# Three-product gate and query tiles, with their lower halves made by transfers or by GpSimd

## The chip, the cores and the metric

The kernel runs on one core of a Trainium2 chip. A core has five engines with queues of their own: TensorE (matrix products, PE in the profile, with PEld for its weight loads), VectorE (DVE), ScalarE (ACT), GpSimd (POOL) and SyncE (SP), whose queue issues transfers. The metric is the device time of one execution in microseconds (us); the time before is the median of three runs.

## The reference, cut to what matters

Two layers, each a mixer block and an expert block, over 16 meta tokens and 256 tokens of width 1024 in float32.

```
def _mixer_block(x, ...):
    h = _rmsnorm(x, mix_g)
    z = h @ w_in                      # conv input, query, kv, rope, gate logits
    u = conv_in[..., :D_CONV] * sigmoid(conv_in[..., D_CONV:])
    u = _causal_depthwise_conv(u, conv_w, conv_b)          # 31 taps, 512 channels
    u = silu(_layernorm(u, conv_ln_g, conv_ln_b))
    y_conv = u @ w_conv_out
    ...                               # multi-head latent attention -> o
    y_mla = o @ w_mla_out
    gates = sigmoid(gate_logits)      # 2 x 1024 columns of z
    merged = gates[..., :D_MODEL] * y_conv + gates[..., D_MODEL:] * y_mla
    return x + merged @ w_out

def _peer(h, wq, keys, u_table, v_table):
    q = (hf @ wq).reshape(T, 8 heads, 2, 128)
    s = einsum('thpd,hpnd->thpn', q, keys)                 # 128 keys each
    sv, si = top_k(s, 16);  top_s, top_pos = top_k(sums of pairs, 16)
    gw = softmax(top_s)
    a = einsum('ted,td->te', u_table[experts], xb)
    return einsum('te,ted->td', gelu(a) * gw, v_table[experts])
```

There are 16,384 experts of width 1024 in each of the tables u and v.

## The kernel before, in words

The program holds the whole model in one run, layer after layer. Layer 0 works on all 272 columns (tokens), layer 1 on the 256 of the output from the mixer's gates on. TensorE takes weights as 128 x 1024 tiles: eight blocks of 128 x 128, one for each 128 rows of the input, against 272 or 256 columns.

**Weights.** They stream in as 1 MB loads of two tiles each, in a list (`srcs`, `raws`), through a ring of buffers `wraw`. `next_w` (L104) hands out the next tile and, at every second one, has SP issue the loads further on in the ring (`dma_to`, L82). `peek_w(n)` (L99) gives a tile that lies n places ahead. In the query stage some loads of the expert table u are taken out of the ring and issued early, at tiles named in `EPLACE` (L35); four of them go into buffers borrowed from mixer tiles (`kh`, `sq`, `g0`, `g1`).

**The two forms of a product.** `ztile` (L298) multiplies a tile in f32: eight matmuls, each of which shows as two in the trace, 16 in all. `three` (L721) has the weight as a sum of two f32r numbers, hi and lo, and the input as xh + xl, and adds the three products hi·xh, lo·xh and hi·xl: 24 matmuls of one pass each. The halves of a weight are made ahead by `high` (L688) and `low` (L713). `high` has ScalarE copy the tile to the type f32r (L709). `low` makes w - hi in one of three ways: by VectorE or GpSimd as a subtraction (L719), or by a transfer, where ScalarE first writes -w rounded the same way (L711) and GpSimd's queue then issues a transfer from w that adds to it (L717). `kinds` (L685) names the buffers of each split tile; they are mixer buffers that are free at that time.

**Order in the mixer.** All engines follow one program text. After the first four tiles come four pairs of conv-input tiles (loop over c, L817), where at c = 2 the normalised input is split into xh (`uk`, L839) and xl, then 16 gate tiles (L859; `TPG`, L29, lists those in three products: 10 to 15), four tiles for y_mla, four for y_conv, and eight of w_out. Attention (`att`) and the convolution are generators, and the text advances them by a fixed number of steps behind each tile: `taps(n, m)` does n conv taps on VectorE (`conv`, L649) and m steps of `conv2` (L665). The 31 taps of a channel block are a multiplication and 30 multiply-adds on VectorE (L661). Of channel block 0 the first KD = 21 taps go another way: ScalarE writes scaled copies, three at a time, accumulating transfers on GpSimd's queue add them up in `part`, and three VectorE additions put them into `acc`. They run as soon as VectorE has begun block 0. `TAPS` (L27) sets the taps of each gate tile. When all taps are done, `layernorm` (L744) starts: sums on VectorE (L747), a product with ones on TensorE, and so on; its steps are placed in the later gate tiles.

**Order in the query stage.** 16 query tiles (L1156) in two-half form from 0 to 11 (tile 16 + i in `parts`; 12 to 15 are f32). Behind the product of a tile the text makes the halves of tiles 3 or 4 ahead (the dictionary at L1163), issues an early load if `EPLACE` has the place, evacuates z to `qr` by ScalarE (L1172), computes the scores of the tile before on TensorE, and picks the best 16 of each by `top16` on VectorE (L1003). From tile 12 on ScalarE copies the scores out (L1029), so TensorE doesn't wait for VectorE's picks. At i = 4 to 11 GpSimd also makes xh, the input of the expert stage (L1205). The steps of `heads(0, 0)` (candidates, exponentials, indices) run in i = 8 to 14 on VectorE; then `numbers` (L1145) computes the expert numbers, and SP moves them to `iww` by `spread` (L1150).

**The expert stage.** 128 tiles of u (product A, L1483) and then 128 of v (product po). Alongside, GpSimd gathers single rows of u by the expert numbers and VectorE reduces them (L1440, L1425); routes come from them through VectorE (L1308) and TensorE transposes (L1319).

Of the kernel before, what the change touches and what calls it, by code (L numbers as in the profile page):

```python
# [7 lines left out]
F32 = mybir.dt.float32  # L8
# [5 lines left out]
OP = mybir.AluOpType  # L14
# [8 lines left out]
KW = 31  # L23
# [3 lines left out]
TAPS = [6, 6, 7, 8] + [9] * 12  # L27
KD = 21
TPG = (10, 11, 12, 13, 14, 15)  # L29
SCALE = 96 ** -0.5  # L30
# [6 lines left out]
MIXQ = {"xg", "uk", "qr", "rq_w", "rq_x", "rq_ym", "tkw0", "tkw1", "tkw2", "tkm", "sk", "scs", "qm",  # L37
        "wq0", "wq1", "seln", "upad", "acc", "sqa", "g0", "g1"}
# [15 lines left out]
def trunk_kernel(ctx: ExitStack, tc: tile.TileContext, a: dict, out: bass.AP, dbg=None, stop=None):  # L54
    nc = tc.nc
# [156 lines left out]
    for l in range(NL):  # L212
# [16 lines left out]
        mixs = ExitStack()  # L229
        mixb = ExitStack()  # L230
        mpa = mixs.enter_context(tc.tile_pool(name=f"mixq{l}", bufs=1))
        mpb = mixb.enter_context(tc.tile_pool(name=f"mix{l}", bufs=1))

        class mp:

            @staticmethod
            def tile(shape, dt, name, **kw):
                return (tw if name in ("sq", "kh", "g0", "g1") else mpa if name in MIXQ else mpb).tile(shape, dt, name=name, **kw)
        zs = ExitStack()
# [425 lines left out]
        def conv2():  # L665

            for k in range(0, KD, 3):
                u_ = mp.tile([128, 3, T], F32, name="cp", bufs=2) if k else part
                for x in range(3):
                    S.activation(u_[:, x, t0:], upad[:, 0, k + x + t0:k + x + T], AF.Copy, scale=weight(0, k + x))  # L670
                    yield
                if k:
                    G.dma_start(part[:, :, t0:], u_[:, :, t0:], accum_op=OP.add)
            for _ in range(2):
                yield
            while ck[0] == KD:
# [3 lines left out]
            yield  # L680

        parts = {}

        xhs_ = []
        kinds = {"g10": 0, "g11": 1, "g12": "k", "g13": 0, "g14": 1, "g15": "s", 0: "k", 1: 0, 2: 1, 3: "s", 4: "k",  # L685
                 19: "k", 20: "a", 21: "q", 22: "w", 23: "s", 24: "q", 25: "a", 26: "s", 27: "w"}

        def high(i, n):  # L688

            w_ = peek_w(n)  # L690
            x = kinds[i] if i in kinds else "aws"[(i - 5) % 3]
            if x == "w":
                hi, lo = [mp.tile([128, 1024], F32, name=f"wq{y}") for y in range(2)]
# [15 lines left out]
            S.activation(parts[i][0], w_, AF.Copy)  # L709
            if i in (21, 23, 25, 27):  # L710
                S.activation(parts[i][1], w_, AF.Copy, scale=-1.0)  # L711

        def low(i):  # L713

            hi, lo, w_ = parts[i]
            if i in (21, 23, 25, 27):
                G.dma_start(lo, w_, accum_op=OP.add)  # L717
            else:
                (G if i in (20, 22, 24, 26) else V).tensor_tensor(lo, w_, hi.bitcast(F32), op=OP.subtract)  # L719

        def three(i, p, xs, wc, cs, first, end, mid=None):  # L721

            hi, lo, _ = parts[i]
            for c in cs:
# [92 lines left out]
        for c in range(4):  # L817
# [17 lines left out]
            if c == 2:  # L835
                xnh = big("uk", [8, T], F32R)
                xnl = mp.tile([128, 8, T], F32, name="un").bitcast(F32R)
                for k in range(8):
                    S.activation(xnh[:, k, t0:], xg[:, k, t0:], AF.Copy)  # L839
# [19 lines left out]
        for i in range(16):  # L859
# [4 lines left out]
            else:  # L864
                z = ztile(t0)
            new = [f"g{i + 2}"] if i + 2 in TPG else []
            ns = [1] if new else []
# [7 lines left out]
            if not ex:  # L875
                todo.append(i)
            if i >= 14:
                high(i - 12, 3)
# [102 lines left out]
        normal(7)  # L981
        mixb.close()
        if stop == f"mix{l}":
            dump(stop, hT)
# [171 lines left out]
        for i in range(16):  # L1156
# [4 lines left out]
            else:  # L1161
                z = ztile(t0)
            for k in {0: (2, 3), 1: (5,), 2: (4,), 3: (7,), 4: (6,), 5: (9,), 6: (8,), 7: (11,), 8: (10,)}.get(i, ()):  # L1163
                high(16 + k, k - i - 1)
                low(16 + k)
            if i in EPLACE:
                k, n = early_[l][EPLACE[i][0]], EPLACE[i][1]
                raws[k] = (two(n).rearrange("p (a b) -> p a b", a=2) if n else
                           ep.tile([128, 2, 1024], F32, name=f"we{i}"))
                nc.sync.dma_start(raws[k], srcs[k])  # L1170
            qT_ = mp.tile([128, T], F32, name="qr", bufs=2)
# [578 lines left out]
```

## Time and profile before

| | us |
|---|---|
| median of three runs (lowest, highest) | 1659.36 (1658.32, 1661.72) |
| the profiled execution | 1659.62 |
| its span | 1657.8 |
| TensorE busy | 1642.4 |
| VectorE busy | 1261.6 |
| ScalarE busy | 693.3 |
| GpSimd busy | 333.0 |

The profiled execution is one run recorded by the hardware. A row of a timeline reads: start and duration in us, engine, line of the program, operation, the written and the read tile, the form; in square brackets how long the engine stood before it and what ended that. A row of the chain of waits has start, duration, engine, tile and line, and the number of instructions. In the windows each engine's busy us stand with its count of instructions, then the granted TensorE clock, the busy share of the 16 transfer engines and the GB/s that they moved. Matmul ends are modelled, and transfers are listed with the median time from issue to landing.

### The profile page before, as it was taken

Reading aid. Unit: us, or ns where it says so; the run is one execution under the profiler, and the core shown is the slowest. Engines: PE = TensorE matmul, PEld = TensorE weight load, DVE = VectorE, ACT = ScalarE, POOL = GpSimd, SP = SyncE. Lnnn points to the kernel's source line nnn. Section 1 sums busy time; section 2 is a strip of 40 time slices with the busy share of each in tenths; the row PEclk is TensorE's granted clock in tenths of the full one; section 3 lists DMA queues with packets and bytes.
Section 4 is the critical chain, followed back from the end, with each engine's and each line's share of the span. In section 5 each row is a group of like instructions: output and inputs, shape, how many; then the busy total and the mean of one; then the engine's idle time right before and its main releaser. Section 6 shows DMA issues by size and latency. Waiting matters only on the chain.

```text
span 1657.8 us, 30712 instructions
## 1 busy us (share of the span) xinstructions
PE 1642.4 (99%) x11827; PEld 1468.5 (89%) x11827; DVE 1261.6 (76%) x3082; ACT 693.3 (42%) x1803; POOL 333.0 (20%) x347
## 2 busy tenths in 40 slices
PE   9999999999999999999999999999999999999999
PEld 7679999999999999999986899999999997566655
DVE  5799899897898544444447998897877886788885
ACT  3565733435554111000024576433445443455554
POOL 0000033221222222222200100432211222233330
PEclk9999999999999999999999999999999999999999
DMA  6444697999999999999962746989999999999994
GB/s 249 113 128 177 242 345 298 424 383 424 416 423 418 424 424 423 424 424 424 417 259 85 176 153 242 340 348 396 362 425 409 409 391 411 420 425 425 424 425 191
DMA packets 86099, 568.52 MB, mean 343 GB/s; under 512 B 10328, under 2 KB 15384, under 8 KB 18744
## 3 DMA queue, kind: packets, MB, share of 16 engines
q1 hardware_dynamic: 50608, 338.51, 50.7%
q0 software_dynamic: 34560, 227.31, 35.0%
q8 instruction: 93, 1.52, 0.4%
q10 hardware_dynamic: 784, 0.74, 0.1%
q14 instruction: 54, 0.44, 0.1%
HBM read 556.18 MB, written 1.05 MB: 336 GB/s over the span
## 4 chain that ended last, share of the span: by engine, by line
PE 87%; DMA 8%; DVE 3%; ACT 1%; issue 1%; POOL 0%; SPq 0%; DVEq 0%; ACTq 0%; POOLq 0%
PE A L62 34%; PE po L62 25%; PE z L62 20%; DMA wraw<-vt 5%; PE aps L62 5%; PE wp L62 2%; DMA X<-vt 2%; DMA sqa<-wraw 1%; DVE acc L661 1%; PE xp L62 0%; PE sc L62 0%; DVE xh L1549 0%; PE wp L1262 0%; DVE tkw L1008 0%; ACT wr L1547 0%
## 5 line engine op out<-in xcount | busy, mean ns | idle before, releaser
L62 PE MATMUL A<-xh,wraw 128*128 128x160 f32 x3520 | 498.0, 300 | 0.0
L62 PEld LDWEIGHTS A<-xh,wraw 128*128 128x128 f32 x3520 | 481.1, 190 | 0.0
L62 PE MATMUL z<-xg,wraw 128*128 128x272 f32 (+2 forms) x832 | 194.1, 392 | 0.0
L1440 DVE SCALAR_TENSOR_TENSOR g<-g,xr 128x1024 f32<-128x1024 f32 x94 | 114.8, 1221 | 90.8 <-DMA g<-uv,iww 90.8
L62 PEld LDWEIGHTS z<-xg,wraw 128*128 128x128 f32 (+1 forms) x832 | 151.8, 189 | 35.0 <-issue 5.8
L1415 POOL DMA_INDIRECT g<-uv,iww x94 | 113.6, 1209 | 306.3 <-DVE va L1425 197.4
L1451 ACT ACTIVATE am<-am 128x1 f32<-128x1 f32 x208 | 40.9, 196 | 312.1 <-DVE g L1440 157.8
L62 PE MATMUL po<-Xh,wraw 128*128 128x160 f32 x1040 | 143.1, 300 | 1.0 <-DMA wraw<-vt 0.9
L62 PEld LDWEIGHTS po<-Xh,wraw 128*128 128x128 f32 x1040 | 141.5, 190 | 2.0 <-DMA wraw<-vt 2.0
L62 PE MATMUL po<-X,wraw 128*128 128x160 f32 x1008 | 138.4, 299 | 1.8 <-DMA wraw<-vt 1.3
L62 PEld LDWEIGHTS po<-X,wraw 128*128 128x128 f32 x1008 | 137.1, 190 | 2.7 <-DMA wraw<-vt 1.0
L1425 DVE SCALAR_TENSOR_TENSOR va<-g,am,va 128x1024 f32<-128x1024 f32 x91 | 116.5, 1281 | 0.3 <-ACT am L1452 0.2
L1340 ACT ACTIVATE ohA<-ohE,wlo 128x128 f16<-128x128 f16 x320 | 105.3, 428 | 5.2 <-DVE ohE L1337 4.4
L1440 DVE SCALAR_TENSOR_TENSOR kh<-kh,xr 128x1024 f32<-128x1024 f32 x48 | 58.6, 1221 | 42.5 <-DMA kh<-uv,iww 42.5
L1440 DVE SCALAR_TENSOR_TENSOR sq<-sq,xr 128x1024 f32<-128x1024 f32 x48 | 58.7, 1222 | 39.4 <-DMA sq<-uv,iww 39.4
L1415 POOL DMA_INDIRECT sq<-uv,iww x48 | 58.0, 1209 | 151.1 <-DVE va L1425 90.6
L1415 POOL DMA_INDIRECT kh<-uv,iww x48 | 59.9, 1248 | 140.4 <-DVE va L1425 92.8
L661 DVE SCALAR_TENSOR_TENSOR acc<-upad,cols,acc 128x272 f32<-128x272 f32 (+1 forms) x198 | 83.0, 485 | 0.2
L1351 ACT ACTIVATE Xh<-wp 128x260 f32<-128x260 f32 (+19 forms) x80 | 24.6, 307 | 131.5 <-DVE Xh L1348 124.8
L1425 DVE SCALAR_TENSOR_TENSOR va<-sq,am,va 128x1024 f32<-128x1024 f32 x48 | 61.5, 1281 | 5.5 <-ACT am L1452 5.5
L1425 DVE SCALAR_TENSOR_TENSOR va<-kh,am,va 128x1024 f32<-128x1024 f32 x48 | 61.5, 1282 | 3.7 <-ACT am L1452 3.7
L1452 ACT ACTIVATE am<-am,iww 128x1 f32<-128x1 f32 x208 | 61.3, 295 | 6.9
(503 smaller groups left out, 3075.0 us busy)
## 6 DMA issues: line engine op xcount, KB each, us to landing
wraw<-u SPq DMA_DIRECT2D x110, 1024.0 KB, 9.2
wraw<-vt SPq DMA_DIRECT2D x109, 1024.0 KB, 12.2
wraw<-w_in SPq DMA_DIRECT2D x27, 1024.0 KB, 4.7
X<-vt SPq DMA_DIRECT2D x17, 1024.0 KB, 11.4
wraw<-wq SPq DMA_DIRECT2D x16, 1024.0 KB, 4.8
we<-u SPq DMA_DIRECT2D x10, 1024.0 KB, 12.1
wraw<-w_out SPq DMA_DIRECT2D x8, 1024.0 KB, 4.6
wraw<-w_mla SPq DMA_DIRECT2D x4, 1024.0 KB, 5.1
```

The lines of the kernel that those rows point to most:

```text
L62: PE.matmul(o, l, r, start=start, stop=stop, skip_group_check=True)
L661: V.scalar_tensor_tensor(acc[:, c, t0:], u_, weight(c, k), acc[:, c, t0:], op0=OP.mult, op1=OP.add)
L1340: S.activation(A_[1][:, t // 2, :, t % 2], E[0][:, t // 2, :, t % 2], AF.Copy, scale=wlo[:, 4 * b + t:4 * b + t + 1])
L1351: S.activation(x_, p[:, :, a:b].rearrange("p t j -> p j t"), AF.Copy, scale=1.0 / WS)
L1415: G.indirect_dma_start(out=g_, out_offset=None, in_=a[f"uv{l}"], in_offset=bass.IndirectOffsetOnAxis(ap=iww[i].bitcast(I32)[:, m // 16, 0, ...
L1425: V.scalar_tensor_tensor(vac[i], r, m_, vac[i], op0=OP.mult, op1=OP.add)
L1440: V.scalar_tensor_tensor(u_, u_, 1.0, xrs[i], op0=OP.mult, op1=OP.mult, accum_out=m_)
L1451: S.activation(m_, m_, AF.Gelu_apprx_tanh)
L1452: S.activation(m_, m_, AF.Copy, scale=iww[i][:, m // 16, 1, m % 16:m % 16 + 1])
```

## The change

- Gate tiles 1, 3, 5 and 7 are computed as three products. Their lower halves are made by transfers. The halves of tiles 1 and 3 are made at conv-input pairs c = 2 and 3, those of 5 and 7 at gate tiles 1 and 3. Tiles 1 and 5 share the buffers `wq0` and `wq1`, tiles 3 and 7 a new one, `gp`.
- For every tile whose lower half a transfer makes (also query tiles 5, 7, 9 and 11, in `parts` as 21, 23, 25, 27), `three` now does all hi·xh first, then all hi·xl, and all lo·xh last.
- KD goes from 21 to 24, so channel block 0 has three more taps by ScalarE and transfers and three fewer on VectorE. The steps of `conv2` in the conv-input loop go from 0, 3, 4, 4 to 0, 4, 5, 5. The three additions of `part` wait until at most 10 taps are left, where before they followed the first taps of block 0.
- Query tiles 12 to 15 are computed as three products too. Their halves are made at i = 9 to 12, the lower one by a GpSimd subtraction.
- The early loads are issued at other places: five at 1, 2, 5, 6, 8 (before 1, 5, 7, 8, 11), the one into `kh` at 4 as before, the one into `sq` at 13 (before 9), and those into `g0` and `g1` at 15 (before 12 and 13), since these two hold the split input of the query tiles, which is now read until tile 15.
- Some small tiles of the query stage come from a pool of their own, `qo`, that is opened when the mixer's buffers are given back; this makes room for `gp`.

```
-KD = 21
-TPG = (10, 11, 12, 13, 14, 15)
+KD = 24
+TPG = (1, 3, 5, 7, 10, 11, 12, 13, 14, 15)
...
-EPLACE = {1: (4, None), 4: (0, "kh"), 5: (5, None), 7: (6, None), 8: (7, None), 9: (1, "sq"), 11: (8, None), 12: (2, "g0"), 13: (3, "g1")}
+EPLACE = {1: (4, None), 2: (5, None), 4: (0, "kh"), 5: (6, None), 6: (7, None), 8: (8, None), 13: (1, "sq"), 15: (2, "g0"), 15.5: (3, "g1")}
+BYDMA = ("g1", "g3", "g5", "g7", 21, 23, 25, 27)
...
-            for _ in range(2):
-                yield
-            while ck[0] == KD:
+            while sum(ck.values()) < 4 * KW - 10:
                 yield
             for x in range(3):
                 V.tensor_add(acc[:, 0, t0:], acc[:, 0, t0:], part[:, x, t0:])
...
+        kinds = {"g1": "v", "g3": "p", "g5": "v", "g7": "p", ... 28: "q", 29: "a", 30: "s", 31: "w"}
...
-            if i in (21, 23, 25, 27):
+            if i in BYDMA:
                 S.activation(parts[i][1], w_, AF.Copy, scale=-1.0)
...
-                (G if i in (20, 22, 24, 26) else V).tensor_tensor(lo, w_, hi.bitcast(F32), op=OP.subtract)
+                (G if i in (20, 22, 24, 26, 28, 29, 30, 31) else V).tensor_tensor(lo, w_, hi.bitcast(F32), op=OP.subtract)
...
+            if i in BYDMA:
+                for w_, x, f, e in ((hi, xs[0], first, None), (hi, xs[1], None, None), (lo, xs[0], None, end)):
+                    for c in cs:
+                        mm(p, w_[:, c * 128:(c + 1) * 128], x[:, c, t0:], c == f, c == e)
+                return
...
-            taps((0, 0, 8, 6)[c], (0, 3, 4, 4)[c], (1, 2, 3)[:max(c, 1)])
+            if c > 1:
+                k = 2 * c - 3
+                high(f"g{k}", 3)
+                low(f"g{k}")
+            taps((0, 0, 8, 6)[c], (0, 4, 5, 5)[c], (1, 2, 3)[:max(c, 1)])
...
+            if i in (1, 3):
+                high(f"g{i + 4}", 3)
+                low(f"g{i + 4}")
...
+            for k in {0: (2, 3), 1: (5,), 2: (4,), 3: (7,), 4: (6,), 5: (9,), 6: (8,), 7: (11,), 8: (10,), 9: (12,),
+                      10: (13,), 11: (14,), 12: (15,)}.get(i, ()):
                 high(16 + k, k - i - 1)
                 low(16 + k)
```

More of the change, by code (lines that the diff above doesn't have):

```diff
@@ L27 @@
 TAPS = [6, 6, 7, 8] + [9] * 12
-KD = 21
-TPG = (10, 11, 12, 13, 14, 15)
+KD = 24
+TPG = (1, 3, 5, 7, 10, 11, 12, 13, 14, 15)
+ONLYQ = {"tkw0", "tkw1", "tkw2", "tkm", "scs", "qm"}
 SCALE = 96 ** -0.5
@@ L34 @@
 EARLY = (0, 1, 2, 3, 8, 10, 12, 14, 16)
-EPLACE = {1: (4, None), 4: (0, "kh"), 5: (5, None), 7: (6, None), 8: (7, None), 9: (1, "sq"), 11: (8, None), 12: (2, "g0"), 13: (3, "g1")}
+EPLACE = {1: (4, None), 2: (5, None), 4: (0, "kh"), 5: (6, None), 6: (7, None), 8: (8, None), 13: (1, "sq"), 15: (2, "g0"), 15.5: (3, "g1")}
+BYDMA = ("g1", "g3", "g5", "g7", 21, 23, 25, 27)
 JS = 63
-MIXQ = {"xg", "uk", "qr", "rq_w", "rq_x", "rq_ym", "tkw0", "tkw1", "tkw2", "tkm", "sk", "scs", "qm",
+MIXQ = {"xg", "uk", "qr", "rq_w", "rq_x", "rq_ym", "sk",
         "wq0", "wq1", "seln", "upad", "acc", "sqa", "g0", "g1"}
@@ L230, in trunk_kernel @@
         mixb = ExitStack()
+        qo = []
         mpa = mixs.enter_context(tc.tile_pool(name=f"mixq{l}", bufs=1))
@@ L237, in tile @@
             def tile(shape, dt, name, **kw):
-                return (tw if name in ("sq", "kh", "g0", "g1") else mpa if name in MIXQ else mpb).tile(shape, dt, name=name, **kw)
+                return (tw if name in ("sq", "kh", "g0", "g1") else qo[0] if name in ONLYQ else mpa if name in MIXQ else mpb).tile(shape, dt, name=name, **kw)
         zs = ExitStack()
@@ L679, in conv2 @@
                 V.tensor_add(acc[:, 0, t0:], acc[:, 0, t0:], part[:, x, t0:])
-            yield
         parts = {}
         xhs_ = []
-        kinds = {"g10": 0, "g11": 1, "g12": "k", "g13": 0, "g14": 1, "g15": "s", 0: "k", 1: 0, 2: 1, 3: "s", 4: "k",
-                 19: "k", 20: "a", 21: "q", 22: "w", 23: "s", 24: "q", 25: "a", 26: "s", 27: "w"}
+        kinds = {"g1": "v", "g3": "p", "g5": "v", "g7": "p", "g10": 0, "g11": 1, "g12": "k", "g13": 0, "g14": 1, "g15": "s", 0: "k", 1: 0, 2: 1, 3: "s", 4: "k",
+                 19: "k", 20: "a", 21: "q", 22: "w", 23: "s", 24: "q", 25: "a", 26: "s", 27: "w", 28: "q", 29: "a", 30: "s", 31: "w"}
         def high(i, n):
@@ L691, in high @@
             x = kinds[i] if i in kinds else "aws"[(i - 5) % 3]
-            if x == "w":
+            if x == "p":
+                t_ = mp.tile([128, 2048], F32, name="gp")
+                hi, lo = t_[:, 0:1024], t_[:, 1024:2048]
+            elif x in ("w", "v"):
                 hi, lo = [mp.tile([128, 1024], F32, name=f"wq{y}") for y in range(2)]
@@ L715, in low @@
             hi, lo, w_ = parts[i]
-            if i in (21, 23, 25, 27):
+            if i in BYDMA:
                 G.dma_start(lo, w_, accum_op=OP.add)
             else:
-                (G if i in (20, 22, 24, 26) else V).tensor_tensor(lo, w_, hi.bitcast(F32), op=OP.subtract)
+                (G if i in (20, 22, 24, 26, 28, 29, 30, 31) else V).tensor_tensor(lo, w_, hi.bitcast(F32), op=OP.subtract)
         def three(i, p, xs, wc, cs, first, end, mid=None):
             hi, lo, _ = parts[i]
+            if i in BYDMA:
+                for w_, x, f, e in ((hi, xs[0], first, None), (hi, xs[1], None, None), (lo, xs[0], None, end)):
+                    for c in cs:
+                        mm(p, w_[:, c * 128:(c + 1) * 128], x[:, c, t0:], c == f, c == e)
+                return
             for c in cs:
@@ L865, in trunk_kernel @@
                 z = ztile(t0)
-            new = [f"g{i + 2}"] if i + 2 in TPG else []
+            new = [f"g{i + 2}"] if i >= 8 and i + 2 in TPG else []
             ns = [1] if new else []
@@ L982, in trunk_kernel @@
         mixb.close()
+        qo.append(mixs.enter_context(tc.tile_pool(name=f"qo{l}", bufs=1)))
         if stop == f"mix{l}":
@@ L1162, in trunk_kernel @@
                 z = ztile(t0)
-            for k in {0: (2, 3), 1: (5,), 2: (4,), 3: (7,), 4: (6,), 5: (9,), 6: (8,), 7: (11,), 8: (10,)}.get(i, ()):
+            for k in {0: (2, 3), 1: (5,), 2: (4,), 3: (7,), 4: (6,), 5: (9,), 6: (8,), 7: (11,), 8: (10,), 9: (12,),
+                      10: (13,), 11: (14,), 12: (15,)}.get(i, ()):
                 high(16 + k, k - i - 1)
                 low(16 + k)
[L1166 to L1170, printed above, removed]
+            for e in (i, i + 0.5):
+                if e in EPLACE:
+                    k, n = early_[l][EPLACE[e][0]], EPLACE[e][1]
+                    raws[k] = (two(n).rearrange("p (a b) -> p a b", a=2) if n else
+                               ep.tile([128, 2, 1024], F32, name=f"we{i}"))
+                    nc.sync.dma_start(raws[k], srcs[k])
             qT_ = mp.tile([128, T], F32, name="qr", bufs=2)
```

## The prediction

> **What bounds the kernel now.** I read the page first, then what TensorE waits for, then the windows around the two places that the change touches, and the timelines there.
>
> ```profile
> span 1657.8 us, 30712 instructions
> PE 1642.4 (99%) x11827; PEld 1468.5 (89%) x11827; DVE 1261.6 (76%) x3082; ACT 693.3 (42%) x1803; POOL 333.0 (20%) x347
> ```
> TensorE is busy for all but 15.4 us. The list of what it waited for is short; of its entries these three matter here (engine, tile, line, what it waited for; total us, times, longest):
>
> ```profile
> PE po L62 <- DMA wraw<-vt: 2.2, 6, 0.7
> ...
> PE z L62 <- DMA sqa<-wraw: 1.7, 1, 1.7
> ...
> PE aps L62 <- DVE zkr L747: 0.7, 1, 0.7
> ```
> The first lies in the expert tables' second half, which the change doesn't reach. The second is one query tile whose lower half came late, the third the layernorm's sum in one gate stage. So the end is set by TensorE's work, and work taken from it counts in full unless a new wait appears. The windows say who is close behind it:
>
> ```profile
> core 0: us, PE busy (x) PEld busy (x) DVE busy (x) ACT busy (x) POOL busy (x), PEclk, DMA share, GB/s
> ...
> 70.00:80.00 10.00, 10.00 (x55) 7.33 (x53) 9.59 (x24) 3.48 (x10) 1.74 (x2) 1.00 0.74 185
> 250.00:260.00 10.00, 9.30 (x61) 7.98 (x60) 9.29 (x51) 2.67 (x12) 0.00 (x0) 1.00 0.12 45
> ...
> 1050.00:1060.00 10.00, 8.33 (x71) 8.14 (x71) 8.23 (x55) 4.00 (x6) 8.18 (x9) 1.00 1.01 308
> ```
> Early in the gates (70 to 80) VectorE is 96% busy and ScalarE has two thirds of its time free. Late in the query stage (1050 to 1060) the transfers are full; at its end (250 to 260) they are nearly idle, and VectorE is busy. The granted clock is 1.00 throughout.
>
> **What is removed: TensorE time.** The chain of waits, in order of time, has runs of equal tiles; an f32 tile is 16 matmuls, a three-product tile 24.
>
> ```profile
> 63.53 7.34 PE z L62 x32
> ...
> 171.20 27.13 PE z L62 x216
> ...
> 921.52 6.91 PE z L62 x32
> ...
> 1005.40 25.53 PE z L62 x216
> ```
> Layer 0: 7.34/2 = 3.67 us for a plain tile, 27.13/9 = 3.01 for a split one, 0.656 saved. Layer 1: 3.455 and 2.837, 0.618 saved. Four gate and four query tiles in each layer change form: 8 x 0.656 + 8 x 0.618 = 5.25 + 4.95 = 10.2 us. Order within a tile doesn't alter the count of matmuls.
>
> **The gate stage.** Does VectorE let TensorE have the time? Its work is a chain from the attention scores to the layernorm sum on which TensorE stalls in layer 1:
>
> ```profile
> 132.60 0.92 DVE L747 TENSOR_TENSOR zkr<-zkr,acc 128x272 f32<-128x272 f32 x2
> 133.87 0.73 PE L62 MATMUL aps<-zkr,ones 128*128 128x272 f32 x2
> 949.57 1.36 DVE L492 TENSOR_REDUCE mx<-aps 128x1 f32<-128x144 f32 x4 [1.98 <-PE aps L62]
> 970.19 0.67 PE L62 MATMUL aps<-zkr,ones 128*128 128x256 f32 x2 [0.67 <-DVE zkr L747]
> L661 DVE SCALAR_TENSOR_TENSOR acc<-upad,cols,acc 128x272 f32<-128x272 f32 (+1 forms) x198 | 83.0, 485 | 0.2
> ```
> The chain's last start that waits for TensorE is the maximum at 949.57. It lies behind all four shorter gate tiles, so it comes 4 x 0.618 = 2.5 us earlier, as TensorE's arrival at the sum does. Behind it VectorE also has three conv taps less (83.0/198 = 0.42 each, 1.26 together); the three closing additions are done before and after. So VectorE is 1.26 earlier relative to TensorE, and the 0.67 stall of layer 1 goes. In layer 0 VectorE ended at 133.52, before TensorE's 133.87, so nothing is lost or won. ScalarE's three extra scaled copies and eight halves go into its free time (6.5 us in the 70 to 80 window alone).
>
> The early splits cost a transfer each. The first, for gate tile 1, is the tight one:
>
> ```profile
> 63.67 2.67 ACT L839 ACTIVATE uk<-xg 128x272 fp32r<-128x272 f32 x8
> 75.72 3.93 PE L62 MATMUL z<-xg,wraw 128*128 128x272 f32 x16
> ...
> 199.28 1.05 ACT L709 ACTIVATE sq<-wraw 128x1024 fp32r<-128x1024 f32 x1
> 200.23 1.05 ACT L711 ACTIVATE sq<-wraw 128x1024 fp32r<-128x1024 f32 x1
> ...
> part<-cp POOLq DMA_DIRECT2D x6, 408.0 KB, 4.3
> ...
> sqa<-wraw POOLq DMA_DIRECT2D x2, 512.0 KB, 11.6
> ```
> ScalarE is free at 66.3; two copies of 1.05 make 68.4; the accumulating transfer lands 4.3 to 11.6 later, at 72.7 to 80.0 (the nearest rows: 408 KB at this place, and 512 KB under full transfers). Gate tile 1 starts at 75.72, and as the lower half is now used last, it needs it 16/24 x 3.01 = 2.0 later, at 77.7. Stall 0 to 2.3 a layer. I take 0, as the window there has 0.74 of the transfers busy and the 4.3 row is from this stage: 512/408 x 4.3 = 5.4, landing at 73.8. Gate tiles 3, 5 and 7 have the time of at least one more tile.
>
> **The query stage.** Two things change: order in the old transfer-made tiles, and four new tiles. The stall in the list above is here, layer 1, query tile 9 (time and length in the chain's row, then TensorE's):
>
> ```profile
> 1046.94 12.58 DMA sqa<-wraw
> ...
> 1059.56 2.99 PE z L62 x23
> ```
> The transfer lands at 1059.52; TensorE had stood since 1057.9 (1059.56 minus 1.67) because the second of the 24 matmuls reads that half. Used last, it is wanted 16/24 x 2.84 = 1.9 later, at 1059.7. The loads issued ahead of it on SP's queue are as many as before up to that time, but for one taken to step 2, some 20 us earlier. So the 1.7 us goes; from below, if the transfer shifts by two, it stays. I take it all, and give 0.3 us back for the end of this stage, by this row:
>
> ```profile
> 1073.73 0.35 ACT L1083 ACTIVATE ew<-ce,rsT 128x64 f32<-128x64 f32 x1 [2.86 <-DVE ce L1082]
> ```
> ScalarE stands 2.86 us before its exponential, for VectorE, in both kernels alike, while TensorE's tiles around it come 0.6 earlier each; tile 12's eviction and the copy for tile 15 are queued behind it. Half of one tile's gain is the allowance, all of 0.6 a layer its upper bound, nothing the lower.
>
> The new lower halves are GpSimd's:
>
> ```profile
> 203.35 2.39 POOL L719 TENSOR_TENSOR sqa<-wraw,acc 128x1024 fp32r<-128x1024 f32 x1 [0.68 <-ACT acc L709]
> ...
> L186 DVE TENSOR_SCALAR rq_yl<-rq_x x4: 295/302/303, 36.5 to 979.0; 128x272 int32<-128x272 int32 x3, 128x256 int32<-128x256 int32 x1
> L186 DVE TENSOR_SCALAR rq_ym<-rq_x x2: 685/736/786, 205.1 to 1037.5; 128x272 int32<-128x272 int32 x1, 128x256 int32<-128x256 int32 x1
> ```
> A copy of 1.05 and a subtraction of 2.39 are 3.4 us, started three tiles (9 us) ahead of use: hidden, with GpSimd's own products for the expert stage ending about there. What they do to VectorE is unknown; the last two rows bound it. The same instruction takes 0.30 us elsewhere and 0.69 to 0.79 when it meets a GpSimd subtraction, 0.43 more. Each subtraction then costs VectorE between 0 and 2.39; I take 0.43, by that row, 1.7 a layer. At the upper end it is 4 x 2.39 = 9.6 a layer, a rival below. The Trainium skill, page "SBUF — State Buffer", section "Who interferes with whom", speaks against the change: a GpSimd operation that reads SBUF and a VectorE operation with two SBUF inputs, or in one of its faster modes, shut each other out for the whole length of an instruction. By that rule the upper end would hold; the rows above show a fifth of it.
>
> **The start of the expert stage.** VectorE works without a break to the end of the routing numbers, and TensorE enters the experts through ScalarE, not through VectorE:
>
> ```profile
> 255.07 0.21 DVE L1145 SCALAR_TENSOR_TENSOR ew<-ef 128x64 int32<-128x64 f32 x1
> 257.09 4.61 PE L62 MATMUL A<-xh,kh 128*128 128x160 f32 x32 [0.59 <-ACT idxT L1036]
> 265.89 1.04 PE L1262 MATMUL wp<-ident,va 128*128 128x128 f32 x8
> 365.88 0.60 PE L1319 MATMUL wp<-ident,ef 128*128 128x128 f32 x4
> 1184.39 0.60 PE L1319 MATMUL wp<-ident,ef 128*128 128x128 f32 x4
> ...
> 358.14 0.28 DVE L1308 SCALAR_TENSOR_TENSOR ef<-ew,ef 128x128 f32<-128x128 f32 x1
> 1179.97 0.29 DVE L1308 SCALAR_TENSOR_TENSOR ef<-ew,ef 128x128 f32<-128x128 f32 x1
> ...
> wraw<-wq SPq DMA_DIRECT2D x16, 1024.0 KB, 4.8
> g<-u SPq DMA_DIRECT2D x4, 1024.0 KB, 10.8
> ```
> So TensorE starts 4 x 0.656 = 2.6 earlier than VectorE's numbers, which (with 1.7 for GpSimd's work) come 4.3 later relative to it; 2.5 + 1.7 = 4.2 in layer 1. The gathers that start from the numbers trail by as much. The first thing that TensorE waits for behind them are the route transposes: at 365.88, with their input ready at 358.42, 7.5 early, and at 1184.39, ready at 1180.26, 4.1 early. Layer 0 has room; layer 1 just holds, with 0.1 to lose.
>
> The third and fourth expert loads now wait on SP behind the routing numbers' transfer, as they need the buffers that query tile 15 reads. Numbers at 255.28 - 257.09 = -1.8, moved by 2.6: U start + 0.8, plus the transfer's issue of about 0.6, so the loads leave at + 1.4. They are used from expert tile 4 on, which follows the transposes of 265.89 + 1.04 = 266.93, at + 9.84. With transfers at 0.12, as the window has it, I take the 4.8 row: landing at + 6.2, no stall. With the 10.8 row + 12.2, a stall of 2.4 a layer, which is kept for the range.
>
> **Sum.** 10.2 + 0.67 + 1.67 - 0.3 = 12.2. The profiled execution took 1659.6 (its span of 1657.8 and 1.8 around it), against a median of 1659.36, so it stands for the median: 1659.6 - 12.2 = **1647.4 us**.
>
> **The rivals.**
> *Gate tile 1 late.* Its lower half lands as the 11.6 row has it, in both layers: 2 x 2.3 = 4.6 back, 1652.0. For it: ScalarE is free only 9 us ahead, and GpSimd issues conv transfers in the same queue. Against: the 4.3 row.
> *The query tiles' time is not kept.* The four new tiles run but half of the query gain, 4 x (0.656 + 0.618) = 5.1, goes to halves that come late behind GpSimd's products, or to gathers that trail: 1652.5 at the whole 5.1. For it: GpSimd 8.18 of 10 at 1050 to 1060. Against: those products end with tile 11.
> *Late expert loads, mild.* The 2.4 above in both layers: 1652.2.
> *Slower: VectorE shut out, and the loads behind it.* Each new subtraction takes its whole 2.39 from VectorE, so the numbers are 9.6 later, and the loads that stand behind them on SP's queue leave at + 11.0, land at + 15.8 (4.8 row) to + 21.8 (10.8 row) against + 9.84: a stall of 6.0 to 12.0 a layer, 1659.4 to 1671.4. It decides from a stall of 6.1 a layer on, where 12.2 is used up. For it: the order on the queue. Against: 0.43 and not 2.39 in the row. The Trainium skill's rule on the shared port speaks for it.
> That the products don't happen as listed I give nothing: the tiles' form is written out.
>
> **How the numbers follow.** Forecast 0.58, gate tile 1 late 0.12, query time lost 0.12, late loads mild 0.06, VectorE shut out 0.12. Of the last, half reaches beyond 1662.7 and half stays in the band of 3.3 us (0.2%, which is about the spread of the three times shown) around 1659.4. So faster 0.58 + 0.12 + 0.12 + 0.06 = 0.88, same 0.06, slower 0.06. The range: below, 1646.0, the forecast without its 0.3 and with the spread of one run (1.1); above, the three cases at 1652 to 1652.5 and a part of two of them together, 1655.0; 0.12 lies above.
>
> **What would show it.** Right: split gate tiles of 3.0 and 2.8 us at places 1, 3, 5, 7, and the same for query tiles 12 to 15; TensorE busy about 1632; the waits for sqa and for zkr gone; no wait at expert tile 4. Wrong in part: a wait on gp or wq0 by gate tile 1; a wait for a transfer into g at expert tile 4; a wait for idxT's transposes around 360 and 1180. Wrong outright: VectorE's rows longer by 2 us in the query stage, and a gap in TensorE of 6 us or more after its first expert tiles 0 to 3.

## The result, and the profile after

The changed kernel took 1673.41 us (median of 6 runs, 1671.95 to 1676.25) against 1659.12 (6 runs, 1656.98 to 1661.72): a ratio of 1.0088, 95% interval 1.0078 to 1.0099. It is 14.3 us slower, where 12.2 us faster was forecast.

The page of the changed kernel, span and engines:

```profile
span 1671.1 us, 31041 instructions
PE 1642.7 (98%) x11955; PEld 1472.8 (88%) x11955; DVE 1263.7 (76%) x3076; ACT 716.4 (43%) x1833; POOL 373.7 (22%) x365
```

TensorE's busy time did not fall by 10 us; it is the same as before (1642.4), and its idle time went from 15.4 to 28.4 us. What it waited for, in the changed kernel (engine, tile, line, what it waited for; total us, times, longest):

```profile
PE z L64 <- ACT g L886: 6.1, 2, 3.5
PE aps L64 <- ACT pr L501: 2.8, 1, 2.8
...
PE sc L64 <- DVE si L1026: 1.4, 2, 1.0
...
PE A L64 <- DMA g<-u: 1.4, 1, 1.4
...
PE aps L64 <- DVE zkr L755: 1.1, 1, 1.1
```

The two largest are new, both for ScalarE: the evacuation of a gate tile, and the attention's exponentials. The wait for sqa of before is gone. Where the time went can be read by stages from TensorE's timelines of the two profiled runs, by the start of gate tile 1, of the layernorm's sum and of the first expert tile in each layer:

| stretch | before | after | difference |
|---|---|---|---|
| start to gate tile 1, layer 0 | 75.72 | 75.88 | +0.2 |
| gate tile 1 to layernorm sum, layer 0 | 58.15 | 67.77 | +9.6 |
| layernorm sum to first expert tile, layer 0 | 123.22 | 121.19 | -2.0 |
| first expert tile to gate tile 1 of layer 1 | 658.43 | 661.69 | +3.3 |
| gate tile 1 to layernorm sum, layer 1 | 54.67 | 59.48 | +4.8 |
| layernorm sum to first expert tile, layer 1 | 116.28 | 113.09 | -3.2 |
| first expert tile to the end | 571.33 | 572.00 | +0.7 |

The loss is in the two gate stages: 14.4 us, where the whole execution lost 13.3. The stretches with the query stages gained 5.2, and the one with layer 0's expert stage gave 3.3 of that back. The windows of layer 0's gate stage, first of the changed kernel, then two of the kernel before (busy us of each engine with its count, then the granted clock, the transfer share, GB/s):

```profile
core 0: us, PE busy (x) PEld busy (x) DVE busy (x) ACT busy (x) POOL busy (x), PEclk, DMA share, GB/s
...
85.00:90.00 5.00, 2.35 (x25) 2.22 (x25) 1.35 (x4) 3.02 (x7) 0.85 (x1) 0.79 0.91 270
90.00:95.00 5.00, 5.00 (x30) 4.71 (x30) 0.00 (x0) 3.90 (x8) 1.72 (x2) 0.87 0.81 154
...
105.00:110.00 5.00, 4.79 (x18) 3.15 (x20) 5.00 (x14) 5.00 (x17) 0.86 (x1) 0.50 0.47 86
110.00:115.00 5.00, 5.00 (x13) 3.25 (x12) 4.97 (x15) 3.52 (x12) 0.00 (x0) 0.50 0.44 84
```

```profile
105.00:110.00 5.00, 5.00 (x35) 4.05 (x34) 5.00 (x15) 3.26 (x11) 0.86 (x1) 1.00 0.01 5
110.00:115.00 5.00, 5.00 (x31) 3.51 (x30) 3.36 (x11) 2.07 (x7) 0.00 (x0) 1.00 0.91 234
```

After each of the two pauses the granted clock is 0.50, for 3.4 and then 10.2 us (a row gives the mean of its window, so 0.79 and 0.87 are part 0.50 and part 1.00). From 105 to 115 TensorE looks almost fully busy and does 31 matmuls where it did 66. The timeline of TensorE in the changed kernel shows each pause (in brackets) and what it drags behind it; the last two rows are the same forms at full clock:

```profile
88.24 2.18 PE L64 MATMUL z<-uk,gp 128*128 128x272 f32 x8 [2.65 <-ACT g L886]
90.22 1.64 PE L64 MATMUL z<-un,gp 128*128 128x272 f32 x8
...
105.21 3.14 PE L64 MATMUL aps<-kh,xh 98*128 98x144 f32 x8 [2.81 <-ACT pr L501]
108.28 2.60 PE L64 MATMUL aps<-t,vt 128*64 128x256 f32 x12
110.81 6.07 PE L64 MATMUL z<-xg,wraw 128*128 128x272 f32 x16
...
121.29 1.57 PE L64 MATMUL aps<-kh,xh 98*128 98x144 f32 x8
122.79 1.45 PE L64 MATMUL aps<-t,vt 128*64 128x256 f32 x12
```

The pauses are 2.65 + 2.81 = 5.5 us. The slow matmuls cost 1.57 + 1.15 + 2.24 = 5.0 behind the second pause (a plain tile takes 3.83 at full clock) and 1.4 behind the first (the same eight take 1.28 and 1.16 in gate tile 1): 6.4 us. So the stretch lost 11.9 against its forecast, and 9.6 + 2.6 = 12.2 is what is missing. More than half of the price of a pause came after it, under the name of busy time.

Why was ScalarE late? Its own timeline in the changed kernel, then GpSimd's:

```profile
78.62 1.35 ACT L673 ACTIVATE cp<-upad,cols 128x272 f32<-128x272 f32 x3 [4.89 <-DMA part<-cp]
86.97 0.93 ACT L673 ACTIVATE cp<-upad,cols 128x272 f32<-128x272 f32 x2 [7.00 <-DMA part<-cp]
87.81 0.37 ACT L886 ACTIVATE g<-z 128x272 f32<-128x272 f32 x1
```

```profile
68.70 1.27 POOL L720 DMA_DIRECT2D wq<-wraw  x1 [67.42 <-ACT wq L714]
69.53 1.39 POOL L676 DMA_DIRECT2D part<-cp  x1
...
78.82 0.85 POOL L676 DMA_DIRECT2D part<-cp  x1 [3.94 <-DMA part<-cp]
87.42 0.85 POOL L676 DMA_DIRECT2D part<-cp  x1 [7.74 <-DMA part<-cp]
```

ScalarE isn't short of time, it stands still. It writes scaled copies for the conv into two buffers, and a buffer comes free only when the transfer that adds it to `part` has landed. Those now land 9.1 and 8.2 us after issue (69.53 to 78.62, 78.82 to 86.97; the median was 4.3 before); the first of them stands right behind the transfer of gate tile 1's half (68.70). Behind the standing copy on ScalarE's queue lies the evacuation of gate tile 0 (87.81), and TensorE, with three buffers for its tiles, stops. ScalarE waited for these transfers 27.3 us in all; in the kernel before no such wait is listed.

### The profile page after: what moved, and what is told of

Read it like the earlier page. It is cut to its first block, busy times and chain, and to the rows that moved or that the text cites. A ratio compares the mean times of both kernels' runs of the same rounds, so it can differ in the third digit from the quotient of the medians.

```text
span 1671.1 us, 31041 instructions
## 1 busy us (share of the span) xinstructions
PE 1642.7 (98%) x11955; PEld 1472.8 (88%) x11955; DVE 1263.7 (76%) x3076; ACT 716.4 (43%) x1833; POOL 373.7 (22%) x365
## 3 DMA queue, kind: packets, MB, share of 16 engines
HBM read 556.18 MB, written 1.05 MB: 333 GB/s over the span
## 5 line engine op out<-in xcount | busy, mean ns | idle before, releaser
L1433 POOL DMA_INDIRECT g<-uv,iww x94 | 122.3, 1301 | 288.6 <-DVE va L1443 189.0
L64 PE MATMUL z<-xg,wraw 128*128 128x272 f32 (+2 forms) x576 | 136.1, 398 | 0.8 <-DMA wraw<-w_in 0.8
L64 PEld LDWEIGHTS z<-xg,wraw 128*128 128x128 f32 (+1 forms) x576 | 105.2, 189 | 28.8 <-issue 5.3
```

Of the source, the lines that this page charges most:

```text
L64: PE.matmul(o, l, r, start=start, stop=stop, skip_group_check=True)
L1433: G.indirect_dma_start(out=g_, out_offset=None, in_=a[f"uv{l}"], in_offset=bass.IndirectOffsetOnAxis(ap=iww[i].bitcast(I32)[:, m // 16, 0, ...
```

## The experiments

**Is it the halves' transfers, or the conv's faster pace?** Two theories were set against each other in the first four runs: A, the transfers of the lower halves slow the conv's accumulations; B, 24 taps at the faster pace outrun them by themselves. First, the halves by GpSimd:

```
-            if i in BYDMA: S.activation(parts[i][1], w_, AF.Copy, scale=-1.0)
+            if i in BYDMA and i not in GATES: ...
-            if i in BYDMA: G.dma_start(lo, w_, accum_op=OP.add)
+            if i in BYDMA and i not in GATES: ...
...
+                (G if i in (20, 22, 24, 26, 28, 29, 30, 31) + GATES else V).tensor_tensor(lo, ...)
```

> The changed kernel, but the lower halves of gate tiles 1, 3, 5 and 7 come from a GpSimd subtraction and not from a transfer. Theory A (the four transfers of halves slow the conv's accumulating transfers, ScalarE stands before a scaled copy, and the gate evacuation behind it holds TensorE): the accumulations are back near 5 us, the waits for g and pr and the half clock go, time 1648 to 1653. Theory B (24 taps at the faster pace outrun the accumulations by themselves): waits of 2 to 3.5 us and the half clock stay, 1665 or more.

Measured: 1668.00 us, ratio 1.0059 (1.0042 to 1.0076). The time is in theory B's range, but not by its waits alone. ScalarE still waited 28.4 us for the accumulations, while TensorE's most costly wait was now for VectorE (`kh` of the attention, 4.2 us in four waits). Something else was new, in VectorE's and GpSimd's timelines of this kernel:

```profile
71.80 4.66 DVE L665 SCALAR_TENSOR_TENSOR acc<-upad,cols,acc 128x272 f32<-128x272 f32 x6
...
77.30 2.40 DVE L665 SCALAR_TENSOR_TENSOR acc<-upad,cols,acc 128x272 f32<-128x272 f32 x5
```

```profile
67.14 4.24 POOL L723 TENSOR_TENSOR wq<-wraw,wq 128x1024 fp32r<-128x1024 f32 x1 [65.86 <-ACT wq L713]
...
72.49 2.42 POOL L723 TENSOR_TENSOR gp<-wraw,gp 128x1024 fp32r<-128x1024 f32 x1
```

Six taps beside a GpSimd subtraction take 4.66 us, where six take 2.56 without one (81.01 in the same timeline) and five 2.40: 2.1 us lost to a subtraction of 2.42. And the subtraction itself can take 4.24, here beside VectorE's split of the input and its first two tap multiplications. As a test of theory A the run was no good, since the substitute had a price of its own.

The pace of before, with the halves' transfers kept:

```
-KD = 24
+KD = 21
-            taps((0, 0, 8, 6)[c], (0, 4, 5, 5)[c], ...
+            taps((0, 0, 8, 6)[c], (0, 3, 4, 4)[c], ...
```

> The changed kernel with 21 taps by transfers at the pace of before (0, 3, 4, 4), the halves of the gate tiles still by transfers. Theory A: the accumulations still take 8 to 9 us and ScalarE still stands, so most of the loss stays, 1662 to 1672. Theory B: the waits go, 1648 to 1653.

Measured: 1672.49 us, ratio 1.0071 (1.0045 to 1.0097), ScalarE's waits 20.9 us. The pace alone is not the cause. By stages the old pace did help: in the profiled execution the gate stage of layer 0 was 4.7 us longer than before instead of 9.6, and that of layer 1 4.5. Another 10.1 us lay in layer 0's expert stage (601.1 us from its first tile to its last, before 591.0), and only part of these can be explained, as said below.

A third buffer for the scaled copies:

```
-                u_ = mp.tile([128, 3, T], F32, name="cp", bufs=2) if k else part
+                u_ = mp.tile([128, 3, T], F32, name="cp", bufs=3) if k else part
```

> The changed kernel with three buffers for the scaled copies where it had two. Both theories have ScalarE's wait for a free buffer as the link to TensorE; if that link is right, one group of three copies more in flight shortens or removes the waits: 1650 to 1665. If ScalarE's own added work is what is late, nothing changes: 1672 to 1675.

Measured: 1663.92 us, ratio 1.0023 (1.0012 to 1.0034); ScalarE's waits fell from 27.3 to 16.6 us. About 9.5 of the loss went with one buffer, so ScalarE's wait for a buffer is a link to TensorE.

**The query part alone.** All that the change does from the query stage on, with gates and conv as before:

```
-KD = 24
-TPG = (1, 3, 5, 7, 10, 11, 12, 13, 14, 15)
+KD = 21
+TPG = (10, 11, 12, 13, 14, 15)
...
-            if c > 1: ... high(f"g{k}", 3); low(f"g{k}")
-            if i in (1, 3): high(f"g{i + 4}", 3); low(f"g{i + 4}")
```

> The kernel before with the query stage's part of the change alone (four more split tiles, order of the products, places of the early loads); gates and conv taps as before. If the whole loss is in the gate stage: 1659.1 - 5.1 (four tiles in two layers) - 1.7 (the stall of query tile 9) + 1 to 3 for the later expert loads = 1653 to 1655. If the query stage loses too: 1658 or more.

Measured: 1658.23 us, ratio 0.9994 (0.9984 to 1.0004): no change that can be told, where 4 to 6 us were expected. The two query stages were as short as in the changed kernel, and the first expert tile came 2.5 and 2.8 us earlier than before, but the end only 1.6 (spans of 1656.2 and 1657.8).

**Halves left out.** The same products with no lower halves made, at the new pace and at the old:

```
+            if i in GATES: parts[i] = parts[i][0], parts[i][0], w_     # in high: no second copy
+            if i in GATES: return                                      # in low: no transfer
```

> The changed kernel at its own pace (24 taps; 0, 4, 5, 5), but the lower halves of gate tiles 1, 3, 5 and 7 are not made: their matmuls read the upper half twice, so the gates differ and the work of TensorE is the same. Theory A (the transfers of the halves are the whole cause): no waits, gate stages 2.6 and 2.5 us shorter than before, 1653 or less. Theory C (the pace of the conv chain and those transfers each suffice: the accumulations land 7 us after issue at the new pace even with the transfer engines less busy, ScalarE stands for them): waits stay, gate stage of layer 0 longer than before by 2 to 6 us, 1660 to 1668.

> As the run before, but with 21 taps by transfers at the pace of before. Both theories: no waits, no half clock, gate stages 2.6 and 2.5 us shorter than before, so with the query stage's part (1658.2 in its own run) 1652 to 1654. If it isn't faster than the query part alone, shorter gate tiles are worth nothing here, whatever the halves cost, because the attention's steps between them set the pace.

Measured: 1657.49 (ratio 0.9988, 0.9979 to 0.9998) and 1655.62 us (0.9977, 0.9968 to 0.9987). So with the halves gone the long waits for ScalarE in the gate stages go, and the half clock behind them: making the halves by transfers cost 16 us at the new pace and 17 at the old, though at the old pace layer 0's expert stage alone differs by 7.5 between the two profiled executions. At the new pace ScalarE still waited 17.2 us for the accumulations, as much as with the third buffer (16.6), and TensorE's longest wait for it in the gates was 0.6 us: a wait costs by what stands behind it, not by its length. But also: four shorter gate tiles a layer, for nothing, bring 0.7 and 2.6 us over the query part alone, not 5.1. In the second of these runs TensorE waits 2.2 us for the layernorm's sum, in the changed kernel 1.1, before 0.7: VectorE is the next in line. Behind the longer of these waits, 1.76 us in layer 1, the clock was 0.50 for 3.4 us.

**The early loads.** In the kernel before, only the two loads moved behind the routing numbers:

```
-... 12: (2, "g0"), 13: (3, "g1")}
+... 15: (2, "g0"), 15.5: (3, "g1")}
```

> The kernel before with one thing changed: the early loads into g0 and g1 are issued at query tile 15, behind the routing numbers' transfer. Theory D (2 MB of loads moved from a time when the transfer engines were idle into the expert stage, where they are full, cost 2 MB / 424 GB/s = 4.9 us of their time and up to that much at the end of layer 0's expert stage): 2 to 6 us slower, 1661 to 1665, with the start of the expert stage where it was. Rival (the loss behind the query part lies in later gathers): 1659.

And in the query part alone, the loads first:

```
                 numbers(ohp["ew"], ohp["ef"], 0)
-                spread(0, 0, nc.sync)
+                late = True
+            if i == 15 and late:
+                late = False
+                spread(0, 0, nc.sync)
```

> The query part alone, with the loads into g0 and g1 ahead of the routing numbers' transfer on SP's queue instead of behind it. They then leave when query tile 15 is done, some 6 us earlier, while the transfer engines are idle. Theory D: most of the 3 us lost behind the query stage in layer 0 and 1 in layer 1 come back, 1653.5 to 1656. Rival (later gathers): as the query part alone, 1657 to 1659.

Measured: 1658.49 us (ratio 0.9994, 0.9985 to 1.0003) and 1655.81 us (0.9979, 0.9969 to 0.9988). Theory D fell with the first: loads moved behind the numbers cost nothing when the numbers themselves come early. In the query part the numbers come 3.3 us after the first expert tile, the loads land too late behind them (waits of 0.7 and 0.4 us before expert tile 4), and with the loads first these waits are gone and the time is 2.4 us less. The waits account for 1.1 of it.

**Two gate tiles instead of four.** On the kernel of the last run:

```
+TPG = (5, 7, 10, 11, 12, 13, 14, 15)
...
+            if i in (1, 3): high(f"g{i + 4}", 3); low(f"g{i + 4}")
```

> The query part with the loads into g0 and g1 first, plus gate tiles 5 and 7 alone in three products, their halves by transfers at gate tiles 1 and 3; 21 taps at the pace of before. Theory A (the halves' transfers slow the conv's accumulations while the transfer engines are full): with two transfers a layer instead of four the full stretch from 70 to 90 us is shorter but the one for tile 5 still falls into it; 1653 to 1662, and what is lost shows as ScalarE's wait for part<-cp. If the accumulations land in about 5 us as before, the two tiles bring up to 2.5: 1653 to 1655.

Measured: 1659.14 us, ratio 0.9994 (0.9983 to 1.0005): the two tiles lose 3.3. ScalarE's waits are 8.0 us and TensorE has no pause over 0.5 us in layer 0's gates, where the stage is 1.3 shorter; in layer 1 it waits 3.5 us for the layernorm's sum, with the clock at 0.50 behind it.

**GpSimd's subtractions in the query stage.** On the same kernel, query tiles 12 to 15 read the upper half twice and nothing is subtracted:

```
+            if i in (28, 29, 30, 31): parts[i] = parts[i][0], parts[i][0], w_
```

> The query part with the loads first, but the lower halves of query tiles 12 to 15 are not made: their matmuls read the upper half twice, so the scores differ and TensorE's work is the same. Theory E (a GpSimd subtraction shuts out VectorE's two-input instructions: some 3 us a layer, as one of 0.22 us took 2.32): the routing numbers come 2 to 3 us earlier after the start of the expert stage, and if the late gathers cost anything there the time falls from 1655.8 to 1653 to 1655; if not, it stays within 0.7 of 1655.8.

Measured: 1655.14 us, ratio 0.9971 (0.9959 to 0.9982), 0.7 below the run with the subtractions, within what their intervals leave. What a subtraction does to VectorE is plain, though. With it, VectorE's rows and GpSimd's:

```profile
244.10 0.23 DVE L1107 SCALAR_TENSOR_TENSOR ab<-nf,ab 128x64 f16<-128x64 f16 x1
244.36 2.32 DVE L1109 SCALAR_TENSOR_TENSOR rm<-ab 128x64 f16<-128x64 f16 x1
246.72 0.22 DVE L1110 SCALAR_TENSOR_TENSOR rm<-rm 128x64 f16<-128x64 f16 x1
```

```profile
244.21 2.39 POOL L725 TENSOR_TENSOR wq<-wraw,wq 128x1024 fp32r<-128x1024 f32 x1 [0.76 <-ACT wq L715]
```

An instruction of 0.22 us takes 2.32, until GpSimd's is over. The picks of the best 16 beside the other three subtractions keep their 0.2 to 0.3 us. The numbers' transfer left 3.3 us after the first expert tile with the subtractions, 0.8 without: 2.5 a layer, between the 1.7 taken and the 9.6 of the upper end. The gathers come that much later, and between these two runs it costs nothing that can be measured.

**All that the runs suggested, together.** The old pace, three buffers, the loads first, on the changed kernel:

> The changed kernel with what the runs so far suggest: 21 taps at the pace of before, three buffers for the scaled copies, and the loads into g0 and g1 ahead of the routing numbers. If ScalarE's wait for a buffer is the whole link, its waits fall below the 16.6 us that the third buffer alone left, the pauses of TensorE and the half clock go, and the time is 1651 to 1656. If the accumulations are simply too slow beside the halves' transfers, a wait of 2 us or more and the half clock stay: 1658 to 1666.

Measured: 1657.38 us, ratio 0.9983 (0.9974 to 0.9992). ScalarE's waits for the accumulations are gone, and TensorE's waits for ScalarE in the gates and the half clock with them, though four transfers of halves a layer run and the first accumulation still takes 9.1 us (69.44 to 78.53). The gate stage of layer 0 is 60.5 us from tile 0 to the sum, as with no halves at all (before: 62.7). Yet it isn't below the run with the loads first and no gate tiles split. In the profiled executions the two gate stages are 3.8 us shorter than in that run, and the stretch from layer 0's first expert tile to gate tile 1 of layer 1 is 3.4 longer; 2.2 of these are one wait, which that run doesn't have. VectorE, ScalarE and TensorE in the composite:

```profile
376.93 1.23 DVE L1462 SCALAR_TENSOR_TENSOR kh<-kh,xr 128x1024 f32<-128x1024 f32 x1 [1.55 <-DMA kh<-uv,iww]
379.28 0.36 DVE L1370 SCALAR_TENSOR_TENSOR X<-wp,X 128x204 f32<-128x204 f32 x1
```

```profile
379.68 0.21 ACT L1373 ACTIVATE X<-wp 128x48 f32<-128x48 f32 x1 [3.23 <-DVE X L1370]
```

```profile
380.41 0.62 PE L64 MATMUL wp<-ohE,ohA 128*128 128x128 f16 x8 [2.22 <-ACT Xh L1373]
```

VectorE stands for a gathered row, its evacuation of the routes comes late behind that, ScalarE's part of it waits, and TensorE waits for ScalarE. The run with the old pace alone has the same chain (3.25 us for the gather, 2.89 for TensorE). Why the gather is late in these two and not in the run with the loads first isn't shown.

**What makes the accumulations slow?** An eighth of the halves' volume, all else kept:

```
-                G.dma_start(lo, w_, accum_op=OP.add)
+                n = 128 if str(i)[0] == "g" else 1024
+                G.dma_start(lo[:, :n], w_[:, :n], accum_op=OP.add)
```

> The changed kernel, but each transfer of a lower half of gate tiles 1, 3, 5 and 7 moves 128 of its 1024 columns, so the rest of the lower half keeps minus the weight and the gates differ; both ScalarE copies, the issue on GpSimd's queue and all orders stay. If the volume is what slows the accumulations: near the run without lower halves, 1657 to 1660. If it is the number of transfers in the queue or ScalarE's second copy: 1668 to 1675.

Measured: 1673.38 us, ratio 1.0083 (1.0067 to 1.0098), waits of 28.4 us. The volume does bear on the accumulation right behind the half: it landed 5.6 us after issue (69.13 to 74.70) instead of 9.1. But the next one, issued at 74.90 and so 0.05 us ahead of a 1 MB weight load, took 8.9, and the time stayed. Theory A in its plain form falls: the volume isn't all of it. Then the two parts of a half, apart and reordered. No transfer, both ScalarE copies:

```
+                if str(i)[0] == "g": return
                 G.dma_start(lo, w_, accum_op=OP.add)
```

> The changed kernel without the four transfers of halves, but with both ScalarE copies for each; the lower half keeps minus the weight, so the gates differ. If ScalarE's second copy alone sets off the waits (it puts the conv's copies 1 us later, and so an accumulation behind a 1 MB weight load): 1667 to 1674. If a transfer of a half in GpSimd's queue is needed, whatever its size: near the run without lower halves, 1656 to 1660.

And the conv's steps ahead of the halves at conv-input pairs 2 and 3:

```
+            taps((0, 0, 8, 6)[c], (0, 4, 5, 5)[c], (1, 2, 3)[:max(c, 1)])
             if c > 1: k = 2 * c - 3; high(f"g{k}", 3); low(f"g{k}")
-            taps((0, 0, 8, 6)[c], (0, 4, 5, 5)[c], (1, 2, 3)[:max(c, 1)])
```

> The changed kernel with one reordering: at conv-input pairs 2 and 3 the conv's steps come ahead of the halves of gate tiles 1 and 3, so ScalarE's scaled copies and the accumulations leave some 2 us earlier. If what counts is whether an accumulation is issued ahead of a weight load and of the halves' transfers: ScalarE's waits shrink by several us and the time falls to 1656 to 1668. If the number of transfers in the stretch counts and not their order: 1670 to 1675.

Measured: 1667.33 us (ratio 1.0047, 1.0032 to 1.0062) and 1668.61 us (1.0050, 1.0032 to 1.0068). One more ScalarE copy of 1.05 us for each half, and no transfer, makes 9.8 of the 16 us. The rows show where. With one copy (halves left out, new pace), GpSimd's accumulations, SP's weight load between them, and ScalarE's wait:

```profile
73.17 0.89 POOL L677 DMA_DIRECT2D part<-cp  x1 [3.97 <-DMA part<-cp]
78.16 0.85 POOL L677 DMA_DIRECT2D part<-cp  x1 [4.09 <-DMA part<-cp]
...
74.88 0.33 SPq L98 DMA_DIRECT2D wraw<-w_in  x1
...
77.72 0.94 ACT L674 ACTIVATE cp<-upad,cols 128x272 f32<-128x272 f32 x2 [3.69 <-DMA part<-cp]
```

With two copies, the same rows:

```profile
74.12 0.89 POOL L676 DMA_DIRECT2D part<-cp  x1 [4.20 <-DMA part<-cp]
83.14 0.85 POOL L676 DMA_DIRECT2D part<-cp  x1 [8.13 <-DMA part<-cp]
...
74.65 0.33 SPq L97 DMA_DIRECT2D wraw<-w_in  x1
...
82.69 0.93 ACT L673 ACTIVATE cp<-upad,cols 128x272 f32<-128x272 f32 x2 [7.72 <-DMA part<-cp]
```

The accumulation is issued 0.95 us later. Instead of 1.7 us ahead of a 1 MB weight load it is 0.5 ahead, and it lands 8.6 us after issue (at 82.7) instead of 4.6 (at 77.7). ScalarE's wait for it is 7.7 us instead of 3.7, which TensorE's buffers no longer cover. (In the kernel before, that load left only at 79.68.) That the place beside the load is what makes the accumulation slow is read from such pairs of rows; no run moved a load alone. Reordering moved the accumulation forward to 71.72, but there it came behind another load, of 70.61, and the half's transfer, and took 10.7 us; gate tile 1's half was then late as well (a wait of 3.05 us).

## Why the prediction was wrong

**The step that failed** is the sentence in which "ScalarE's three extra scaled copies and eight halves go into its free time" and cost nothing. The cover was named as 6.5 us of free time in a window of 10. Those were gaps between instructions with dates: each scaled copy needs a buffer that a transfer gives back, and the gate evacuations and exponentials stand behind the copies in order. The accumulations, for which the page of before has 4.3 us, took 9.1 and 8.2: the first behind the transfer of one half, the second behind that of another (74.03) and a weight load (75.36). With the copies alone, where no half was transferred, a delay of 1 us that put an accumulation 0.5 us ahead of a load made one as slow (8.6). ScalarE's waits grew to 7 us, and they passed to TensorE. In the two gate stages the forecast was -5.8 us (5.1 and the 0.67 stall) and the outcome +14.4.

**The price of a pause** was in no step. The text counted only stalls; behind pauses of 2.65, 2.81 and 3.47 us the clock was halved, and this returned 6.4 us to TensorE's busy time in layer 0 and, counted the same way, 2.7 in layer 1. In the kernel before, its longest pause between matmuls, 1.67 us, left the clock at 1.00, so nothing there showed it. The length of a pause doesn't decide it alone: 1.76 us (halves left out, old pace) and 2.04 us (halves left out, new pace) were followed by 0.50, and 1.90 us (old pace) and 1.99 us (third buffer) weren't. The Trainium skill's page "TensorE: Matmul & The Clock Gate", section "Part 1: The HAM clock gate", describes this: the clock drops to half after a window of about 3.4 us without work. The traces agree on the half (0.50), and the three stretches at half clock in the changed kernel lasted 3.4, 10.2 and 6.8 us; they differ on the pause that it takes, as 2.65 us was enough there and 1.76 us in another run.

**The stall at the layernorm's sum** was to go, and stayed: 1.06 us in layer 1 of the changed kernel, 1.29 with the halves left out at the new pace, 1.76 at the old. The working let VectorE's chain come 2.5 us earlier together with TensorE, from the wait of 1.98 us at 949.57 on. With the halves left out at the old pace that wait is gone, and VectorE's rows have none at all from 934.6 to the sum: shorter tiles can't bring it further forward there. So its own work takes back part of what four shorter gate tiles are worth. In that run the stretches from gate tile 1 to the sum are 2.2 and 1.0 us shorter than before, where 2.6 and 2.5 were taken for the tiles alone.

**The tiles** were priced rightly: query tile 12 took 2.9 us in layer 1 (1083.14 to 1086.05), and gate tile 1 of layer 0 took 3.2 at full clock (75.88 to 79.08), where the plain tile took 3.9 (75.72 to 79.58). **The stall of query tile 9** went as worked out. **The query stages** gained 2.0 and 3.2 us against 2.6 and 2.5 + 1.7; of the missing 1.6, 1.4 is the wait for `si` in the list above, VectorE not yet done with scores that ScalarE doesn't copy out, which the working had left out.

**Gate tile 1 late**, the first of the rivals, did not happen in the changed kernel: its half was there in time, and the transfer that was late was the conv's. **The loads at expert tile 4** waited 1.37 us in layer 0:

```profile
276.05 9.03 PE L64 MATMUL A<-xh,g 128*128 128x160 f32 x64 [1.37 <-DMA g<-u]
```

The working took the numbers at U start + 0.8 for the loads, though it had them 1.7 later for the gathers; they came at + 3.3. **VectorE shut out**, the slower rival, was half right in its mechanism (2.5 us a layer, an instruction held for the whole of GpSimd's) and wrong in its weight; the final time was slower for another reason. The row from which 0.43 was taken had been misread as a fifth of an exclusion. In the kernel before it is

```profile
205.12 0.79 DVE L186 TENSOR_SCALAR rq_ym<-rq_x 128x272 int32<-128x272 int32 x1
```

and the subtraction beside it runs from 203.35 to 205.74: the instruction began 0.62 us before the subtraction's end and was over 0.17 after it, so the row has room for no more than the rest of that subtraction. The Trainium skill's rule in "SBUF — State Buffer", section "Who interferes with whom", was better than that reading: the conv taps, with two inputs in SBUF, and the 2.32 row are as it says. The picks were not held.

**Not settled:** layer 0's expert stage took longer in every variant with the new query stage, by 0.7 (loads first) to 10 us (old pace) from its first expert tile to its last. Single waits explain part: 1.4 at expert tile 4 in the changed kernel; 2.2 behind a late gather in the composite; with the old pace 1.9 at expert tile 4, 1.6 at the route transposes and 2.9 behind a late gather. The rest is open. The transfer engines are full there in all kernels (0.99 to 1.01 in every 50 us from 350 to 800), so a gain before it may be taken back by them, but no run shows it by itself. Nor was it tried what makes an accumulation slow beside a load or a half's transfer.

The best kernel found that leaves nothing out is the query part with the loads first, 1655.81 us, ratio 0.9979 to the kernel before. It leaves the gate tiles alone.

## What to carry to other kernels

Free time on an engine covers new work only if nothing queued behind that work has a date: for each added instruction, follow the in-order queue to the next one that another engine waits for, and ask what a buffer or a transfer in between does when it is 1 us late. A chain of transfers that just fits between larger loads is such a place, and one more buffer can cover it. An engine that hardly waits for another gains little when that one gets faster: here VectorE had 2 us of such a wait left, and used them up. Where TensorE is the bound, a pause of 2.7 us can cost twice itself, and the profile books the second half as busy time: look at the clock and at the count of matmuls in a window before believing a busy share.

## What the runs showed of the hardware

- Pauses of TensorE of 2.65, 2.81 and 3.47 us were followed by a granted clock of 0.50 for 3.4, 10.2 and 6.8 us. Below that the runs differ: 1.76 and 2.04 us were followed by 0.50 in two runs, 1.67, 1.90 and 1.99 us by 1.00 in three others.
- A 408 KB accumulating transfer of GpSimd's queue landed 4.6 us after issue when issued 1.7 us ahead of a 1 MB weight load, and 8.6 us after when 0.5 us ahead. Behind a half's transfer of 512 KB on the same queue it took 9.1, behind one of an eighth of that 5.6.
- A GpSimd subtraction of 2.39 us held a VectorE instruction of 0.22 us for 2.32; six conv taps beside one took 4.66 instead of 2.56 us, and a subtraction beside VectorE's split of the input and its first tap multiplications took 4.24. VectorE's picks of the maximum beside the same subtractions kept their 0.2 to 0.3 us.
